# Mixture-of-experts stage: places in the token table by expert instead of by group, sorting and bringing back in sets of four experts

## The chip, the cores and the metric

The kernel runs on one core of one Trainium2 chip. Its time is the device time of one execution in microseconds (us). The core has a matrix engine (TensorE, in the profile PE for the matmuls and PEld for loading their stationary operand), VectorE (DVE), ScalarE (ACT), GpSimd (POOL) and SyncE (SP). Here SP issues nearly all loads of weights from HBM.

## The reference: what is computed

Two layers on 512 tokens of width 1024. A layer is a mixer (retention, differential attention and gated linear attention side by side, then an output projection) and a mixture of experts, both gated and added to the residual X. The change is in the mixture of experts alone:

```
def route(h, router_w, router_b):
    scores = sigmoid(h @ router_w);  biased = scores + router_b          # 32 experts in 8 groups of 4
    g_sel = argmax over groups of the sum of the group's 2 best biased scores
    idx = the 2 best experts inside that group;  gates = their scores, normalised
def moe(h, idx, gates, w_gate, w_up, w_down):                            # 1024x512, 1024x512, 512x1024 per expert
    u = silu(x_e @ w_gate[e]) * (x_e @ w_up[e])
    y_e = (u @ w_down[e]) * gates
    out[token] += y_e
```

All of it is fp32. An expert has 6 MiB of weights, so a layer reads 192 MiB for its 32 experts. With the inputs of the reference the eight groups of the first layer hold 115, 96, 85, 71, 54, 46, 31 and 14 tokens, those of the second 108, 105, 94, 64, 50, 41, 30 and 20. Ranked by their tokens, the experts of ranks 1, 6, 7, 16, 17 and 32 hold 82, 54, 49, 32, 29 and 1 in the first layer, and 93, 55, 47, 28, 27 and 3 in the second.

## The kernel before

**Routing.** `route(i)` finds the group of each token of tile i (four tiles of 128 tokens), `weigh(i)` the two experts and their gates. Matmuls with a triangle and with ones count the tokens of each group ahead of each token (`pc`), and a chain on VectorE ranks the eight groups by count. The four largest get 128 places each, the others 64: 768 places.

**Sorting the rows.** `Pt` is a 0/1 matrix of tokens by places. The normalised tokens, split in a rounded part `xh` and the rest `xl`, are multiplied by it: for each of two halves of the places (384 columns) and each of eight k, eight matmuls with 128x128 of `xh` or `xl` as the stationary operand, whose columns are read with a step of four elements (line 1358). The result `hs` stands for all places before the first expert starts.

**Experts.** A list `WHERE` sets their order: an expert of a large group (wide) and one of a small group (narrow) by turns. A wide expert's weights are split in two fp32r parts (a cast on ScalarE, a subtraction on VectorE: `split`), and each product is three fp32r matmuls (`three`), 72 of 512 columns per expert. A narrow expert takes fp32 weights as they are, and two 64-wide matmuls stand side by side in the array (`halved`); an fp32 matmul has two records in the trace. In the loop over experts, `gate_part(e+1)`, `down_part(e)` and `up_part(e+1)` follow each other, and after each quarter of one of these `step()` runs one step of what waits in the queue `apart`.

**Bringing back.** The four experts of a group add into one PSUM sum `ya`. After the fourth, `combine` scales it, splits it in two fp32r parts, and multiplies it by the transposed 0/1 matrix (built on VectorE from `srow`), eight small steps of two matmuls or four of four, which `step()` puts between the expert matmuls.

**Weights.** SP issues 1 MiB per DMA (line 1435), in the order in which the experts use them, into eight slots (two `ring`, four `wm`, two that are first `pre` and later `late`), each when its last reader is done with it. Instructions of the expert loop are recorded by a helper, line 122, so that line 122 stands for all of them.

**Rest.** If a group has more tokens than places, a loop after the experts takes the others in blocks of 128; with these inputs there are none.

Of the kernel before, what the change touches and what calls it, by code (L numbers as in the profile page):

```python
# [29 lines left out]
NWIDE = 4  # L30
CAPS = (128,) * NWIDE + (64,) * (NG - NWIDE)
OFFS = tuple(sum(CAPS[:r]) for r in range(NG))
PLACES = sum(CAPS)

WHERE = [(r, j) for w in range(NWIDE) for j in range(4) for r in (w, w + NWIDE)]
WHERE[-4:] = [(NWIDE - 1, 2), (NWIDE - 1, 3), (NG - 1, 2), (NG - 1, 3)]


def _constants():
    c, a = {}, {}  # L40
# [8 lines left out]
    c["ranks"] = np.broadcast_to(np.arange(8.0), (128, 8))  # L49
    c["scol"] = np.stack([OFFS[r] + p % CAPS[r] for r in range(8)], 1)  # L50
    c["caps"] = np.broadcast_to(np.array(CAPS, np.float64), (128, 8))
# [26 lines left out]
    a["places"] = np.broadcast_to(np.arange(float(PLACES // 2)), (128, PLACES // 2))  # L78
# [61 lines left out]
def hybrid_trunk(ctx: ExitStack, tc: tile.TileContext, x, c, positions, w_mod, b_mod, norm1_g, norm2_g, w_in,  # L140
# [89 lines left out]
    xmid = dr.tile([S, D])  # L230
# [138 lines left out]
    for l in range(depth):  # L369
        first = l == 0  # L370
        with ExitStack() as ps:
# [712 lines left out]
            places = rx.tile([128, PLACES // 2])  # L1084
            SP.dma_start(places, catt[:, AOFF["places"][0]:sum(AOFF["places"])])
# [26 lines left out]
            gate, grp = rt.tile([128, NT, NE]), p3.tile([128, NT, NG])  # L1112
# [14 lines left out]
            def route(i):  # L1127
# [14 lines left out]
                else:  # L1142

                    for n in range(2):
# [31 lines left out]
                V.tensor_scalar(grp[:, i], cst("gidx"), r1, None, op0=OP.is_equal)  # L1176

                T.matmul(pc[:, (i + 1) * NG:(1 + NT) * NG], cst("ones"),
                         grp[:, i, None, :].to_broadcast([128, NT - i, NG]), start=(i == 0), stop=False)
# [3 lines left out]
            def weigh(i):  # L1183
# [12 lines left out]
                V.scalar_tensor_tensor(two, two, IMM, sc, op0=OP.is_equal, op1=OP.mult)  # L1196
# [34 lines left out]
            for i in range(NT):  # L1231
                acc[i] = out_bank(i)
                second(i, 0)
                if i:
                    turn_x(i - 1, 1)
                    logits(i - 1, 0)
                turn_x(i, 0)
                second(i, 1)
                if i:
                    logits(i - 1, 1)  # L1240
                residual(acc[i], i, 1)
                SP.dma_start(xmid[i * 128:(i + 1) * 128], X[:, i])
# [10 lines left out]
            drain(ahead_, route(NT - 1))  # L1253


            gf = grp.rearrange("p i g -> p (i g)")
            T.matmul(pc[:, 0:NG], cst("ustrict"), gf[:, 0:NG], start=False, stop=False)
            T.matmul(pc[:, NG:NT * NG], cst("ustrict"), gf[:, NG:], start=False, stop=True)
# [4 lines left out]
            def over_groups(a, axis=1):  # L1263
                return a[:, None, :].to_broadcast([128, NG, NG]) if axis else a[:, :, None].to_broadcast([128, NG, NG])

            key, cmp_, rank = pt_([128, NG]), pt_([128, NG, NG]), pt_([128, NG])
            V.scalar_tensor_tensor(key, pc[:, NT * NG:(1 + NT) * NG], float(NG), cst("gidx"), op0=OP.mult, op1=OP.add)
            V.tensor_tensor(cmp_, over_groups(key), over_groups(key, 0), op=OP.is_gt)
            V.tensor_reduce(rank, cmp_, axis=AX.X, op=OP.add)

            at_rank, og, perm = pt_([128, NG, NG]), pt_([128, NG, NG]), pt_([128, NG])
            V.tensor_tensor(at_rank, over_groups(rank), over_groups(cst("ranks"), 0), op=OP.is_equal)
            V.tensor_tensor(og, at_rank, over_groups(cst("ranks")), op=OP.mult)
            V.tensor_reduce(perm, og, axis=AX.X, op=OP.add)
            permi = rt.tile([1, NG], I32)
            V.tensor_copy(permi, perm[0:1])

            tmp, tmp2 = pt_([128, NT, NG]), pt_([128, NT, NG])
            nth, rk, aw, cap, over, slot = [pt_([128, NT]) for _ in range(6)]
            V.tensor_mul(tmp.rearrange("p i g -> p (i g)"), pc[:, 0:NT * NG], gf)  # L1280
            V.tensor_tensor(tmp2, grp, rank[:, None, :].to_broadcast([128, NT, NG]), op=OP.mult)
            V.tensor_reduce(nth, tmp, axis=AX.X, op=OP.add)
            V.tensor_reduce(rk, tmp2, axis=AX.X, op=OP.add)
            V.tensor_scalar(cap, rk, NWIDE - 0.5, CAPS[-1] - CAPS[0], op0=OP.is_gt, op1=OP.mult)
            V.tensor_scalar(aw, rk, float(NWIDE), 0.0, op0=OP.subtract, op1=OP.max)
            V.tensor_scalar(cap, cap, float(CAPS[0]), None, op0=OP.add)
            V.scalar_tensor_tensor(aw, aw, CAPS[-1] / CAPS[0] - 1.0, rk, op0=OP.mult, op1=OP.add)
            V.tensor_tensor(over, nth, cap, op=OP.is_ge)
            V.scalar_tensor_tensor(slot, aw, float(CAPS[0]), nth, op0=OP.mult, op1=OP.add)
            slots = rt.tile([128, NT])  # L1290
            V.scalar_tensor_tensor(slots, over, 4.0 * S, slot, op0=OP.mult, op1=OP.add)
            Pt = rx.tile([128, NT, PLACES], F32R)
            HP = PLACES // 2
            slot2 = pt_([128, NT])
            V.tensor_scalar(slot2, slots, -float(HP), None, op0=OP.add)
            for c, of in enumerate((slots, slot2)):
                for i in range(NT):
                    V.tensor_scalar(Pt[:, i, c * HP:(c + 1) * HP], places, of[:, i:i + 1], None, op0=OP.is_equal)
            drain(weigh(NT - 2), weigh(NT - 1))

            gate4 = rt.tile([128, NT, 4])
            V.tensor_reduce(gate4, gate.rearrange("p i (g e) -> p i e g", e=4), axis=AX.X, op=OP.add)

            behind = rt.tile([128, NT])
            V.tensor_sub(nth, nth, cap)
            V.scalar_tensor_tensor(nth, rk, float(S), nth, op0=OP.mult, op1=OP.add)
            V.scalar_tensor_tensor(nth, nth, 1.0, over, op0=OP.add, op1=OP.mult)
            V.tensor_scalar(behind, nth, -1.0, None, op0=OP.add)
            nbi = rt.tile([1, NG + 1], I32)
            cnt, nbf, nbt = [pt_([128, NG]) for _ in range(3)]  # L1310
            V.tensor_tensor(og, at_rank, over_groups(pc[:, NT * NG:(1 + NT) * NG]), op=OP.mult)
            V.tensor_reduce(cnt, og, axis=AX.X, op=OP.add)
            V.tensor_sub(cnt, cnt, cst("caps"))
# [4 lines left out]
            V.tensor_copy(nbi[:, 0:NG], nbf[0:1])  # L1318
            V.tensor_reduce(nbt[:, 0:1], nbf, axis=AX.X, op=OP.max)
            V.tensor_copy(nbi[:, NG:NG + 1], nbt[0:1, 0:1])  # L1320
# [13 lines left out]
            npre = 2  # L1334
            after = {}

            def pre_done():

                spre.close()
                pre.clear()  # L1340
                wn = after["pool"] = pool(spre, f"wn{l}", "right")
                after["gt2b"] = wn.tile([128, D])
                A.dma_start(after["gt2b"], bcast(mods[l, 5 * D:6 * D], D))
                after["gt2h"] = wn.tile([128, 512])
                for n in range(2):
                    A.dma_start(after["gt2h"][64 * n:64 * n + 64], bcast(mods[l, 5 * D + 512 * n:5 * D + 512 * n + 512], 512, 64))
# [3 lines left out]


            hs = wm.tile([128, KD, PLACES])
            for c in range(2):
                for k in range(KD):
                    b = pbank("x", 3)[:, 0:HP]
                    for i in range(NT):
                        for n, xx in enumerate((xh, xl)):
                            T.matmul(b, xx[:, i].rearrange("p (q t k) -> p q k t", q=2, k=4)[:, k // 4, k % 4],
                                     Pt[:, i, c * HP:(c + 1) * HP], start=(i == 0 and n == 0), stop=(i == NT - 1 and n == 1))
                    dst = hs[:, k, c * HP:(c + 1) * HP]  # L1360
                    if k % 2:
                        V.tensor_scalar(dst, b, hcol[:, 0, k:k + 1], hcol[:, 1, k:k + 1], op0=OP.mult, op1=OP.add)
                    else:
                        A.activation(dst, b, AF.Identity, scale=hcol[:, 0, k:k + 1], bias=hcol[:, 1, k:k + 1])

            def window(r):

                nwin[0] += 1
                xT = wm.tile([128, 2, KD, 128], F32R, tag="exT")
                w = slice(OFFS[r], OFFS[r] + 128)  # L1370
                for h in ((0, 4), (4, 8)) if nwin[0] == 1 else ((0, 8),):
                    ks = slice(*h)
                    A.copy(xT[:, 0, ks], hs[:, ks, w])
                    V.tensor_sub(xT[:, 1, ks], hs[:, ks, w], xT[:, 0, ks])
                return xT

# [403 lines left out]
```

## Time and profile before

| | |
|---|---|
| time, median of 3 runs | 1844.78 us (1844.6 to 1845.76) |
| profiled execution: its time, its span | 1843.05 us, 1841.2 us |
| mean granted TensorE clock | 0.981 |
| PE busy | 1765.0 us (96%) |
| DVE, ACT busy | 1095.8 us (60%), 784.2 us (43%) |
| read from HBM | 501.73 MB |

The span is from the first to the last instruction; the execution's own time is 1.85 us longer. Busy time of PE has modelled ends, so that a busy PE is not PE at its peak. The mixture of experts takes about 550 us of each layer: from 419 to 971 us in the first, and from 1287 us to the end in the second.

### The profile page before, as it was taken

Reading aid. Unit: us, or ns where it says so; the run is one execution under the profiler, and the core shown is the slowest. Engines: PE = TensorE matmul, PEld = TensorE weight load, DVE = VectorE, ACT = ScalarE, POOL = GpSimd, SP = SyncE. Lnnn points to the kernel's source line nnn. Section 1 sums busy time; section 2 is a strip of 40 time slices with the busy share of each in tenths; the row PEclk is TensorE's granted clock in tenths of the full one; section 3 lists DMA queues with packets and bytes.
Section 4 is the critical chain, followed back from the end, with each engine's and each line's share of the span. In section 5 each row is a group of like instructions: output and inputs, shape, how many; then the busy total and the mean of one; then the engine's idle time right before and its main releaser. Section 6 shows DMA issues by size and latency. Waiting matters only on the chain. (4 is left out here: it accounts for less than half of the span.)

```text
span 1841.2 us, 28185 instructions
## 1 busy us (share of the span) xinstructions
PE 1765.0 (96%) x10891; PEld 1270.0 (69%) x10892; DVE 1095.8 (60%) x1968; ACT 784.2 (43%) x1207; POOL 89.4 (5%) x136
## 2 busy tenths in 40 slices
PE   5999999989999999999998999997999999999997
PEld 3866767768665666665748887986966666666673
DVE  3646664464547557566655778656455846756664
ACT  3344442343534443444523555443344444444350
POOL 1010000020000000000000110112000000000000
PEclk9999999998999999999998999998999999999998
DMA  9565547416999999999964211131789999999994
GB/s 333 166 213 191 171 160 226 164 73 253 359 423 378 392 423 367 415 422 353 423 247 141 70 46 47 54 124 51 308 358 422 369 403 422 367 415 419 362 420 179
DMA packets 115617, 512.12 MB, mean 278 GB/s; under 512 B 14978, under 2 KB 42896, under 8 KB 66320
## 3 DMA queue, kind: packets, MB, share of 16 engines
q1 hardware_dynamic: 111952, 504.93, 70.6%
q0 software_dynamic: 1072, 3.32, 0.5%
q10 hardware_dynamic: 2448, 1.94, 0.4%
q8 instruction: 90, 1.47, 0.3%
q14 instruction: 55, 0.45, 0.1%
HBM read 501.73 MB, written 8.42 MB: 277 GB/s over the span
## 5 line engine op out<-in xcount | busy, mean ns | idle before, releaser
L122 DVE TENSOR_TENSOR H<-R,H 128x1024 fp32r<-128x1024 f32 x368 | 431.4, 1221 | 108.9 <-ACT H L122 108.4
L122 ACT CAST H<-R 128x1024 fp32r<-128x1024 f32 x368 | 363.8, 1048 | 47.5 <-DMA R<-in_w_down_dram 28.7
L579 PEld LDWEIGHTS a<-H,u 128*128 128x128 f32 x1728 | 216.5, 190 | 45.0 <-issue 42.2
L579 PE MATMUL a<-H,u 128*128 128x256 f32 x1728 | 245.7, 290 | 0.0
L122 PE MATMUL y<-H,euT 128*128 128x512 f32 x768 | 188.4, 399 | 1.0 <-DVE euT L122 1.0
L122 PE MATMUL g<-H,exT 128*128 128x512 f32 x720 | 183.9, 402 | 0.0
L122 PE MATMUL u<-H,exT 128*128 128x512 f32 x720 | 177.1, 400 | 0.0
L122 PEld LDWEIGHTS y<-H,euT 128*128 128x128 f32 x768 | 141.6, 188 | 46.1 <-ACT H L122 9.2
L122 PEld LDWEIGHTS u<-H,exT 128*128 128x128 f32 x720 | 132.6, 188 | 54.3 <-issue 22.5
L122 PEld LDWEIGHTS g<-H,exT 128*128 128x128 f32 x720 | 131.4, 188 | 36.1 <-issue 8.5
L122 DVE SCALAR_TENSOR_TENSOR eu<-u,u,es 128x256 f32<-128x256 f32 (+1 forms) x62 | 37.9, 612 | 190.3 <-PE u L122 190.3
L122 PE MATMUL g<-R,u 128*64 128x256 f32 x1024 | 126.8, 386 | 0.0
L122 PE MATMUL y<-R,euT 128*64 128x512 f32 x512 | 121.2, 602 | 1.1 <-ACT euT L122 1.1
L122 PE MATMUL u<-R,u 128*64 128x256 f32 x1024 | 118.9, 383 | 0.0
L122 DVE TENSOR_TENSOR u<-u,x 128x512 f32<-128x512 f32 x128 | 84.4, 684 | 45.7 <-PE x L122 45.4
L122 PEld LDWEIGHTS u<-R,u 128*64 128x64 f32 x1024 | 70.1, 137 | 45.3 <-issue 13.9
L122 ACT COPY euT<-x 128x256 f32<-128x256 f32 x32 | 11.9, 373 | 209.9 <-PE x L122 189.3
L122 PEld LDWEIGHTS g<-R,u 128*64 128x64 f32 x1024 | 66.9, 136 | 46.3 <-issue 15.4
L122 PE MATMUL x<-eyh,ePT 128*128 128x512 f32 (+1 forms) x256 | 75.1, 460 | 9.2 <-DVE u L122 5.8
L122 ACT CAST euT<-x 128x512 fp32r<-128x512 f32 x32 | 18.7, 584 | 150.6 <-PE x L122 150.5
L122 PEld LDWEIGHTS y<-R,euT 128*64 128x64 f32 x512 | 32.3, 136 | 63.6 <-issue 52.2
L122 PEld LDWEIGHTS x<-eyh,ePT 128*128 128x128 f32 (+1 forms) x256 | 33.7, 192 | 51.2 <-DVE u L122 31.0
(597 smaller groups left out, 2289.4 us busy)
## 6 DMA issues: line engine op xcount, KB each, us to landing
R<-in_w_gate_dram SPq DMA_DIRECT2D x128, 1024.0 KB
R<-in_w_up_dram SPq DMA_DIRECT2D x128, 1024.0 KB
R<-in_w_down_dram SPq DMA_DIRECT2D x128, 1024.0 KB
M<-in_w_mod_dram SPq DMA_DIRECT2D x80, 512.0 KB
R<-in_w_in_dram SPq DMA_DIRECT2D x20, 1024.0 KB
slab<-in_w_mod_dram SPq DMA_DIRECT2D x16, 512.0 KB
R<-in_w_in_dram SPq DMA_DIRECT2D x24, 256.0 KB
R<-in_w_out_dram SPq DMA_DIRECT2D x4, 1024.0 KB
```

Source lines behind the costliest of these rows:

```text
L122: return self.tc.keep_in_program_order(f(*args, **kw))
L579: T.matmul(acc[i // 2][:, i % 2], a[q][:, k, tk], hl[:, w, k], start=(i % 2 == 0 and q == 0 and k == 0 and n3 == 0), stop=(i % 2 == 1 and ...
```

## The change

Places are given to experts, not to groups. The 32 experts are ranked by their tokens; the six largest get 128 places each, the next ten 64 and the last sixteen 32. They stand in eight sets of four, `(128, 32, 64, 32)` six times and `(64, 32, 64, 32)` twice, and are computed in that order. The table of places before was one matrix of 768 columns for all; now it is one of 256 (or 192) columns for each set, made by `select(s)` while the first expert of the set ahead of it is at work. An expert with 32 places uses four 32-wide matmuls side by side. The sums of a 128- or 64-place expert are scaled and split right after it (`finish`), those of four 32-place experts are put together in four blocks; `combine(s)` then adds all the blocks of a set in one PSUM sum for each tile of tokens. The weights have six slots (`ring` and `wm`) after three first ones (`pre`) are given up.

```
-NWIDE = 4
-CAPS = (128,) * NWIDE + (64,) * (NG - NWIDE)
+SETS = ((128, 32, 64, 32),) * 6 + ((64, 32, 64, 32),) * 2
...
-            drain(ahead_, route(NT - 1))
+            drain(chained(ahead_, weigh(NT - 2)), chained(route(NT - 1), weigh(NT - 1)))
...
+            V.tensor_scalar(cmp_, krow, kcol, None, op0=OP.is_gt)
+            V.tensor_reduce(rank, cmp_, axis=AX.X, op=OP.add)
+            V.tensor_scalar(at_rank, cst("ranks")[0:NE], rank, None, op0=OP.is_equal)
+            b = bt()
+            T.matmul(b[0:1, 0:NE], cst("pidx")[0:NE], at_rank, start=True, stop=True)
...
+                T.transpose(b[0:NE, i * 128:(i + 1) * 128], place[:, i], ident)
+            A.copy(placeT, b[0:NE])
...
+                T.matmul(b[:, i * NE:(i + 1) * NE], placeT[:, i * 128:(i + 1) * 128], at_rank, start=True, stop=True)
+            V.tensor_scalar(placeR.rearrange("p i e -> p (i e)"), b[:, 0:NT * NE], BIG, None, op0=OP.add)
...
-            npre = 2
+            npre = 3
...
-            hs = wm.tile([128, KD, PLACES])
-            for c in range(2):
-                for k in range(KD):
...
+            def select(s):
...
+                for _, cap, o, r in mine:
+                    V.tensor_tensor(Pt[:, :, o:o + cap], cst("iota")[:, None, 0:cap].to_broadcast([128, NT, cap]),
+                                    placeR[:, :, r:r + 1].to_broadcast([128, NT, cap]), op=OP.is_equal)
+                yield
...
+                for k in range(KD):
+                    b = pbank("x", 3)[:, 0:w]
+                    for i in range(NT):
+                        for n, xx in enumerate((xh, xl)):
+                            T.matmul(b, xx[:, i].rearrange("p (q t k) -> p q k t", q=2, k=4)[:, k // 4, k % 4], Pt[:, i, 0:w],
+                                     start=(i == 0 and n == 0), stop=(i == NT - 1 and n == 1))
...
+                    yield
...
+                        for h in range(128 // cap):
+                            T.matmul(b[cap * h:cap * (h + 1), j:j + 1], Pt[:, i, o:o + cap].bitcast(F32), gateR[:, i, r:r + 1],
...
-                place = oldest("R8", [("ring", nr), ("wm", mr_)] + [("pre", npre)] * len(pre) + [("late", lr)] * len(late))
+                place = oldest("R8", [("pre", npre)] * len(pre) + [("ring", nr), ("wm", mr_)])
...
+            def apart_(out, a, cap, columns, start, stop, turned_=0):
+                n = 128 // cap
+                for h in range(n):
+                    w = columns((h - turned_) % n)
+                    T.matmul(out[cap * h:cap * (h + 1), 0:w.shape[-1]], a, w, start=start, stop=stop)
...
+            def step():
+                for todo in (later, ahead_of):
+                    if todo and next(todo[0], todo) is todo:
+                        todo.popleft()
...
+            def places_of(cap, which, n):
+                b = pbank("x", 3)
+                T.matmul(b, which, prow, start=True, stop=True)
+                PT = after["pool"].tile([128, NT, 128], F32R, tag=f"PT{n}")
...
+                V.tensor_scalar(PT.rearrange("p i t -> p (i t)"), b, cst("scol")[:, j:j + 1], None, op0=OP.is_equal)
...
+            def combine(s):
+                yield from of_quarters(s)
+                for i in range(NT):
+                    add(done[s], i)
+                    yield
...
-            src = _Ahead(pieces(items), lambda: 4)
+            src = _Ahead(pieces(items), lambda: 1)
...
+                if e % 4 == 0 and s + 1 < len(SETS):
+                    ahead_of.append(select(s + 1))
...
+                if e % 4 == 3 and e + 1 < ne:
+                    later.append(combine(s))
```

The first place is on PE, inside the down product of the first 128-place expert (`y`, weights `H`). Before, four runs of six matmuls follow each other there, and the narrow expert's up product (`u`, 64 wide) comes next:

```order
L122 MATMUL y_4699<-H_866_4704,euT_4723 128x512 x6
L122 MATMUL y_4699<-H_867_4711,euT_4723 128x512 x6
L122 MATMUL y_4699<-H_871_4728,euT_4723 128x512 x6
L122 MATMUL y_4699<-H_872_4735,euT_4723 128x512 x6
L122 MATMUL u_4781<-R_875_4751,u_817_4385 64x256 x8
```

Now, in the same product, a burst of `select` for the set after (`x` from `Pt`, with `xh` and `xl` as the two stationary operands by turns) stands between two runs of six, and so on through the product and through the 32-place expert's gate and up ahead of it and behind it:

```order
L128 MATMUL y_4769<-H_873_4744,euT_4717 128x512 x6
L128 MATMUL x_4779<-Pt_4681,u_685_3812 128x256
L128 MATMUL x_4779<-Pt_4681,u_686_3813 128x256
L128 MATMUL x_4779<-Pt_4681,u_685_3812 128x256
L128 MATMUL x_4779<-Pt_4681,u_686_3813 128x256
L128 MATMUL x_4779<-Pt_4681,u_685_3812 128x256
L128 MATMUL x_4779<-Pt_4681,u_686_3813 128x256
L128 MATMUL x_4779<-Pt_4681,u_685_3812 128x256
L128 MATMUL x_4779<-Pt_4681,u_686_3813 128x256
L128 MATMUL y_4769<-H_877_4770,euT_4717 128x512 x6
```

The sorting moved from ahead of all experts into the first expert of each set, eight matmuls at a time.

The second place is on PE too, where the sums of a set come back: what is new is a burst for one tile of tokens (`yh` the scaled sums of a 128-place and of a 64-place expert, `PT` their transposed 0/1 matrices) inside the next set's first 32-place gate (`g`, 32 wide):

```order
L128 MATMUL g_5326<-R_962_5301,hs_4696 32x128 x8
L128 MATMUL x_5335<-yh_893_4876,PT_902_4965 128x512
L128 MATMUL x_5336<-yh_898_4905,PT_902_4965 128x512
L128 MATMUL x_5335<-yh_893_4876,PT_902_4965 128x512
L128 MATMUL x_5336<-yh_898_4905,PT_902_4965 128x512
L128 MATMUL x_5335<-yh_934_5138,PT_937_5153 128x512
L128 MATMUL x_5336<-yh_934_5138,PT_937_5153 128x512
L128 MATMUL x_5335<-yh_934_5138,PT_937_5153 128x512
L128 MATMUL x_5336<-yh_934_5138,PT_937_5153 128x512
L128 MATMUL g_5326<-R_962_5301,hs_4696 32x128 x8
```

Before, such a burst came once per group, not per set, and had two matmuls (wide) or four (narrow); now it has eight, and 16 in every second set, with the 32-place blocks.

## Rows read from the trace of the kernel before

**Rows 1.** The page: span.
```profile
span 1841.2 us, 28185 instructions
```

**Rows 2.** Windows, first layer: routing, sorting, experts, end; length, then busy us by engine, clock, DMA share, GB/s.
```profile
399.60:418.90 19.30, 7.19 (x44) 6.28 (x42) 13.93 (x76) 5.45 (x12) 5.41 (x5) 0.69 0.07 28
418.90:454.00 35.10, 35.01 (x150) 33.26 (x150) 15.20 (x40) 10.49 (x16) 3.04 (x4) 0.93 0.66 263
454.00:958.40 504.40, 500.97 (x2662) 325.82 (x2661) 304.40 (x327) 222.91 (x271) 0.00 (x0) 1.00 0.96 386
958.40:971.00 12.60, 4.94 (x17) 2.23 (x16) 9.98 (x19) 8.29 (x21) 0.00 (x0) 0.69 0.29 80
```

**Rows 3.** Windows: one stretch amid the experts at full load.
```profile
500.00:520.00 20.00, 20.00 (x109) 12.86 (x105) 12.53 (x12) 10.40 (x13) 0.00 (x0) 1.00 1.01 423
```

**Rows 4.** Groups by form, PE, 400 to 980 us: busy us, mean ns of one.
```profile
L122 PE MATMUL y<-H,euT 128*128 128x512 f32 x384 | 94.2, 399 | 0.5 <-DVE euT L122 0.5
L122 PE MATMUL g<-H,exT 128*128 128x512 f32 x360 | 91.9, 402 | 0.0
...
L122 PE MATMUL g<-R,u 128*64 128x256 f32 x512 | 63.4, 386 | 0.0
L122 PE MATMUL y<-R,euT 128*64 128x512 f32 x256 | 60.6, 602 | 0.5 <-ACT euT L122 0.5
...
L1358 PE MATMUL x<-u,u 128*128 128x384 f32 x128 | 31.6, 411 | 3.2 <-DVE u L1298 3.2
L122 PE MATMUL x<-eyh,ePT 128*128 128x512 f32 x64 | 22.2, 428 | 0.0
L122 PE MATMUL x<-u,eu 128*128 128x128 f32 x96 | 18.5, 302 | 0.5 <-DVE eu L122 0.2
L122 PE MATMUL x<-eyh,ePT 64*128 64x512 f32 x64 | 15.2, 486 | 4.9 <-DVE u L122 3.1 <-ACT eyh L122 1.4 <-DVE eyh L122 0.3
...
L1609 PE MATMUL x<-u,u 4*64 4x4 f32 x16 | 0.6, 197 | 0.0
```

**Rows 5.** Timeline on PE: two runs of 32-wide matmuls; start us, us.
```profile
118.23 0.62 PE L695 MATMUL l<-QF,KF 128*32 128x128 f32 x16
118.67 0.61 PE L322 MATMUL m<-M,u 128*32 128x256 f32 x8
```

**Rows 6.** Timeline on ACT and DVE: two results of the sorting one after the other.
```profile
441.27 0.67 ACT L1364 ACTIVATE u<-x,u 128x384 f32<-128x384 f32 x1 [3.06 <-PE x L1358]
443.14 0.68 DVE L1362 TENSOR_SCALAR u<-x,u 128x384 f32<-128x384 f32 x1 [3.06 <-PE x L1358]
```

**Rows 7.** Groups by form, PEld, 400 to 980 us.
```profile
L122 PEld LDWEIGHTS y<-H,euT 128*128 128x128 f32 x384 | 70.8, 188 | 23.0 <-ACT H L122 4.6 <-DVE euT L122 1.8 <-issue 1.2
L1358 PEld LDWEIGHTS x<-u,u 128*128 128x128 f32 x128 | 31.3, 330 | 3.4 <-issue 3.3
L122 PEld LDWEIGHTS x<-u,eu 128*128 128x128 f32 x96 | 15.0, 205 | 9.3 <-issue 4.6 <-DVE eu L122 1.8 <-DVE u L122 1.1
```

**Rows 8.** The page's groups: fp32r matmuls of 256 columns in the mixer.
```profile
L579 PE MATMUL a<-H,u 128*128 128x256 f32 x1728 | 245.7, 290 | 0.0
```

**Rows 9.** Timeline on PE: a burst of bringing back between 64-wide matmuls.
```profile
936.49 0.73 PE L122 MATMUL x<-eyh,ePT 128*128 128x512 f32 x2
937.16 1.08 PE L122 MATMUL g<-R,u 128*64 128x256 f32 x8
938.17 0.73 PE L122 MATMUL x<-eyh,ePT 128*128 128x512 f32 x2
```

**Rows 10.** Timeline, the last tile's group on DVE, and the first sorting matmul.
```profile
414.04 0.23 DVE L1176 TENSOR_SCALAR u<-u,r 128x8 f32<-128x8 f32 x1
...
418.99 0.68 PE L1358 MATMUL x<-u,u 128*128 128x384 f32 x1 [3.19 <-DVE u L1298]
```

**Rows 11.** Timeline, from the last expert's sum to the next layer's first matmul.
```profile
958.46 0.69 DVE L122 TENSOR_TENSOR es<-y,u 128x512 f32<-128x512 f32 x1 [7.25 <-PE y L122]
...
971.69 0.58 PE L450 MATMUL t<-at,u 128*128 128x128 f32 x1 [5.43 <-DVE at L429]
```

More of the change, by code (lines that the diff above doesn't have):

```diff
@@ L28, with _order @@
 START = GV, DQ, DK
[L30 to L36 removed]
+SETS = ((128, 32, 64, 32),) * 6 + ((64, 32, 64, 32),) * 2
+KINDS = (128, 64, 32)
+BIG = 1024.0
+def _order():
+    ex = [(s, n, c) for s, cs in enumerate(SETS) for n, c in enumerate(cs)]
+    rank = {e[:2]: r for r, e in enumerate(sorted(ex, key=lambda e: (-e[2], e[:2])))}
+    return [(s, c, sum(SETS[s][:n]), rank[s, n]) for s, n, c in ex]
+ORDER = _order()
+CAPS = [c for s, c, o, r in sorted(ORDER, key=lambda e: e[3])]
 def _constants():
@@ L1273, in hybrid_trunk @@
[L1273 to L1281, printed above, removed]
@@ L1289, in hybrid_trunk @@
[L1289 to L1298, printed above, removed]
@@ L1299, in hybrid_trunk @@
[L1299 to L1313, printed above, removed]
+            ccol, kcol, krow, rank, cmp_, at_rank = [pt_([NE, n]) for n in (1, 1, NE, 1, NE, NE)]
+            V.tensor_copy(ccol, b[0:NE, 0:1])
+            V.scalar_tensor_tensor(kcol, ccol, float(NE), cst("pidx")[0:NE], op0=OP.mult, op1=OP.subtract)
@@ new lines, in hybrid_trunk @@
+            b = bt()
+            for i in range(NT):
+                T.matmul(b[:, i * NE:(i + 1) * NE], gateT[:, i * 128:(i + 1) * 128], at_rank, start=True, stop=True)
+            V.tensor_copy(gateR.rearrange("p i e -> p (i e)"), b[:, 0:NT * NE])
+            prow, oner = rt.tile([NE, S], F32R), rt.tile([NE, NE], F32R)
+            b = bt()
+            T.matmul(b[0:NE], at_rank, placeT, start=True, stop=True)
+            A.copy(prow, b[0:NE])
+            G.tensor_copy(oner, ident[0:NE, 0:NE])
@@ L1341, in pre_done @@
                 wn = after["pool"] = pool(spre, f"wn{l}", "right")
[L1342 to L1346, printed above, removed]
+                for c_ in KINDS:
+                    w, m = D * c_ // 128, 128 // c_
+                    for a_ in range(m if c_ == 32 else 1):
+                        g_ = after[c_, a_] = wn.tile([128, w])
+                        for n in range(m):
+                            o = 5 * D + w * ((n - a_) % m)
+                            A.dma_start(g_[c_ * n:c_ * (n + 1)], bcast(mods[l, o:o + w], w, c_))
@@ new lines, in select @@
+                    yield
+                b = pbank("x", 3)[:, 0:4]
+                for j, (_, cap, o, r) in enumerate(mine):
+                    for i in range(NT):
+                        for h in range(128 // cap):
+                            T.matmul(b[cap * h:cap * (h + 1), j:j + 1], Pt[:, i, o:o + cap].bitcast(F32), gateR[:, i, r:r + 1],
+                                     start=(i == 0 and j == 0), stop=(i == NT - 1 and j == len(mine) - 1))
+                gc = gcols[s] = wm.tile([128, 4], tag="gc", bufs=2)
@@ L1556, in combine_last @@
+            def combine(s):
+                yield from of_quarters(s)
+                for i in range(NT):
+                    add(done[s], i)
+                    yield
+                del done[s]
+            def combine_last(s):
                 if l + 1 < depth:
                     preload("natural_log_exp_and_others")
-                PT = back(r)
-                yfs = [gain_y(ya, n, wm.tile([128, 512], tag=("es", "eu")[n]), wide_) for n in range(2 if wide_ else 1)]
-                yhs = [parts(yf) for yf in yfs]
+                for _ in of_quarters(s):
+                    pass
@@ new lines, in hybrid_trunk @@
+                            for i in range(NT):
+                                G.tensor_scalar(diag[:, i], ident, ob[:, i:i + 1], None, op0=OP.mult)
+                            b = pbank("x", 3)
+                            T.matmul(b, cst("ones"), diag.rearrange("p i t -> p (i t)"), start=True, stop=True)
+                            PTb = after["pool"].tile([128, NT, 128], F32R, tag="PT0")
+                            V.tensor_scalar(PTb.rearrange("p i t -> p (i t)"), b, cst("pidx"), None, op0=OP.is_equal)
@@ new lines, in hybrid_trunk @@
+                            for q in range(4):
+                                T.transpose(b[:, q], u_.rearrange("p (q t k) -> p q k t", q=2, k=2)[:, q // 2, q % 2], ident)
+                            ub = wm.tile([128, 2, KD, 128], tag="exT")[:, 0, 0:4]
+                            A.copy(ub, b)
+                            ya = pbank("y", 1, [128, 2, 512])
+                            for q, raw in enumerate(raws(w_down)):
+                                for k in range(2):
+                                    for n in range(2):
+                                        T.matmul(ya[:, n], ub[:, 2 * q + k], raw[:, k * D + n * 512:k * D + n * 512 + 512],
+                                                 start=(q == 0 and k == 0), stop=(q == 1 and k == 1))
@@ L1740, in hybrid_trunk @@
+                            yhs = []
+                            for n in range(2):
+                                yf = after["pool"].tile([128, 512], tag="eyf")
+                                V.tensor_mul(yf, ya[:, n], after[128, 0][:, n * 512:(n + 1) * 512])
+                                yhs.append(parts(yf, f"yh0{n}"))
+                            for i in range(NT):
+                                add([(128, PTb, yhs)], i)
                 if l + 1 < depth:
```

419 lines of the change are left out of this document (200 added, 219 removed).

## Prediction

> **What bounds the kernel now.** I began with the windows by stage [rows 2]. The reader is to see that a layer's experts take 504.4 us, and that PE is busy for 501.0 of them at full clock while the DMA engines are at 0.96. Nothing idles there that could be given back; DVE (304) and ACT (223) have room. The second thing to see is how close the loads are: at full load 423 GB/s [rows 3], so 1 MiB in 2.48 us, and the 192 pieces of a layer in 476 us. The sorting ahead of the experts is 35.1 us of PE, during which the slots fill and the loads then stop (263 GB/s). So the change has to be read as a bill on PE, with the loads as a floor some 60 us under the present sum of sorting and experts (539.5 us). All sums are made against the profiled execution, 1843.05 us with a span of 1841.2 [rows 1], 0.1% under the median of the runs shown.
>
> **The bill on PE, per layer.** Groups by form give each price [rows 4]; a group's busy time holds the modelled ends of its runs, so differences under some 10 us are not to be trusted.
>
> - *Experts.* A 128-place expert has three parts of 24 matmuls: 94.2/16 = 5.9 us for down, 91.9/15 = 6.1 for gate (up stands between them), 18.0 in all. A 64-place one has 4.0 (63.4/16) and 3.8 (60.6/16), 11.6 in all. For 32 places the nearest row is the mixer's 32-wide run [rows 5]: 16 records, which are two groups of four fp32 matmuls of 128 columns, in 118.67 - 118.23 = 0.44 us, so 0.22 per k. Gate and up have eight k, down has four of twice the columns: 3 x 1.76 = 5.3, with run ends 5.6. Ten 128-place experts go (-180), six 64-place ones go (-70), sixteen of the new kind come (+90): **-160**. Bounds of the new kind: 5.3, and 8.8 if their weight columns, which gate and up read with a step of two, come at half the rate: -165 to -109. I stay near the low end, because transposes read their stationary operand with that step and pay little for it (load 205 ns against 188 [rows 7]).
> - *Sorting.* 128 matmuls become 8 sets x 64 = 512. Columns fall from 384 to 256 each, but I don't think that helps. Two results of eight matmuls come 1.87 us apart [rows 6], 0.234 us per matmul, though a 512-column matmul of the experts costs 94.2/384 = 0.245. What stands behind it is the load of the stationary operand with its step of four: 330 ns mean against 188, and busy 31.3 of the 31.6 us [rows 4, 7]. So each of the 512 costs 0.247 still (31.6/128): 126 us, **+95**. The lower bound is the fp32r matmul of 256 columns with a contiguous operand, 245.7/1728 = 0.142 [rows 8]: 73 us, +41.
> - *Bringing back.* Per layer 96 matmuls of 128 rows at 0.245 (23), 160 of 64 rows at 15.2/64 = 0.24 at most and half of that where two run side by side (30), 128 of 256 columns at 0.142 (18): 72, less the present 22.2 + 15.2: **+34** (+20 to +45).
> - *Placement and gates.* 32 new matmuls of 512 columns spread each expert's places over the rows: **+8**. The gates of the places come from 352 matmuls of one column, 704 records at 0.6/16 = 0.037 as the 64-wide ones there: 26, less about 4 now: **+22** (+10 to +30). Transposes fall from 96 to 60 at 0.19: **-7**.
> - *Visits.* Each burst between matmuls of another tile width costs something beside its matmuls: from 937.16 to 938.83 (938.17 and the two matmuls' 0.66) pass 1.67 us for eight records of 0.124 and two of 0.245, which leaves 0.19 [rows 9]. Visits go from 48 to about 120 (56 of sorting, 28 of bringing back, 32 of placement, 7 of gates): **+14**, and a first strided load that nothing hides in each burst of sorting makes it **+18** (+10 to +30).
>
> The sum is **+10 us per layer on PE** (-70 to +85, were all bounds to go one way). The saving in experts is eaten by sorting.
>
> One rule speaks on the largest term. The Trainium skill (TensorE: Matmul & The Clock Gate, LDWEIGHTS) gives the load of a stationary operand as columns over 1.2 GHz, an estimate of 107 ns for 128 columns whatever their step; by it the sorting would be no dearer than the contiguous row and the sum -44. The same skill (Advanced Engine Details and Errata, SBUF Cachelines) says that accesses need two hits on a 16-byte line for full speed, which a step of four fp32 misses and a step of two keeps; the 330, 205 and 188 ns of the trace agree with this one.
>
> **The slots.** DVE, ACT and SP lose work or have room: 120 splits fewer a layer. What does not even out is the order. All sorting, and nearly all of bringing back, falls to the first expert of a set. Call A the stretch of gate(32), down(128), up(32) in a set: 9.5 us of experts, 8 x 1.87 of sorting, visits 2.4, gates 3, transposes and placement 2, and bringing back 4 x 2 us, in every second set 6 more: about 41 us. Its loads are 15 us, and then six slots are full. The next three iterations take 3.9 + 1.8 + 3.9, 1.8 + 3.8 + 1.8 and 6.1 + 1.8 + 5.9 = 31 us on PE; of their 18 pieces six lie ready and twelve have to come, 12 x 2.48 = 30 us, after the first slot is freed and with the way from issue to use, about 33. PE then waits 2 us at least; since the loads lag most on the short 32-place parts and are ahead again only in A, I take 4 us for each of eight sets: **+32 per layer** (0, if the slots cover it, to +64). Before, a wide and a narrow expert by turns took 18.0 + 11.6 = 29.6 us for 29.8 us of loads, with eight slots: nothing to even out.
>
> **Both ends.** The routing now waits for `weigh` and then goes six times between PE, DVE and ACT (counts, rank, transposes, regrouping, 0/1 matrix) where it went twice: 414.04 to 418.99 now [rows 10]; I take **+5** (+2 to +9). After the last expert, four placements, eight small casts and four bursts of 16 matmuls follow, against four bursts of four: 958.46 to 971.69 now [rows 11], **+7** (+3 to +12). ACT issues 19 gain loads where it issued three, in the first expert: **+1**.
>
> Per layer 10 + 32 + 5 + 7 + 1 = +55, for two layers +110: 1843 + 110 = 1953, on the scale of the runs **1955 us**.
>
> **Rivals.**
> *The loads, not PE, set the stage, and it is faster.* The mechanism is the sorting's matmul: at the contiguous 0.142 us each set's A falls by 6 us and the set comes nearer to its loads. That gives 55 - 54 = +1 per layer, and with even sets no waits for slots, -31: 1843 - 62, about 1780. It decides at 0.14 us per sorting matmul if the waits stay, at 0.20 if they go. For it: the columns do fall by a third. Against it: busy 31.3 of 31.6 us of loads, which 256 columns don't shorten. Chance 0.09. The LDWEIGHTS rule of the Trainium skill (TensorE: Matmul & The Clock Gate), weighed above, would have it so.
> *PE alone counts.* The six slots cover A's unevenness: 55 - 32 = +23 per layer, 1890. For it: the loads had 0.04 to spare on average. Against it: eight slots become six while the sets become uneven. Chance 0.25.
> *The forecast*, 1955, own range 1915 to 2000: chance 0.50.
> *Worse.* Waits at their upper bound and 32-place weights at half rate: +32 + 50 more per layer, about 2100; either alone 2020 to 2055. Chance 0.12.
> *It does not do what it says.* Were an expert to have more tokens than places, the block loop would run with 6 MiB loaded beside nothing, 15 us of loads plus its matmuls, 30 us or more for each; the counts of the inputs leave three places at the tightest rank (29 of 32), so it stays empty. What is left, 0.04, is a change of no size.
>
> **How the numbers follow.** The likeliest case gives 1955. The range 1870 to 2015 takes in the case of PE alone and the forecast, and part of the worse one; 0.1 stays out below and 0.1 above. A measurement of this kernel tells about 0.2% from no change. Faster 0.10, within 0.2% 0.03, slower 0.87.
>
> **What would show it.** Sorting: 512 matmuls a layer at 0.23 to 0.25 us, their loads busy nearly all of it; at 0.14 my largest term is wrong. The 32-place parts: 1.8 us each without interruption. The windows: PE near 100% and DMA well under 0.9 in each A, then DMA at 1.0 and PE with gaps that weights end in the three iterations behind it; a stage with PE full throughout is the second rival. The experts with their sorting should take 580 us where sorting and experts take 539.5 now. Wrong altogether would be a stage near 500 us with DMA at 1.0.

## The result and the profile after

The changed kernel takes **2160.61 us** (median of 4 runs, 2154.89 to 2162.45) where the kernel before takes 1844.69 us (1842.37 to 1845.76): ratio 1.171, 95% interval 1.169 to 1.173. It is slower, as forecast, but by 316 us where I said 110, and far outside the range. The profiled execution takes 2154.89 us, its span is 2153.0 us. The page, with the line on the core's clock, shows PE busy for longer, at a smaller share of the span, and at a lower granted clock (before: 1765.0 us, 96%, 0.981):

```profile
span 2153.0 us, 39387 instructions
PE 1907.8 (89%) x16315; PEld 1396.0 (65%) x16316; DVE 1030.2 (48%) x2278; ACT 645.0 (30%) x1215; POOL 95.4 (4%) x186
...
core 0: 2153.0 us, clock 0.925
```

The windows of the first layer, in the columns of [rows 2]: routing, from the first sorting matmul to the last down product, and the end. Then the first set in three pieces: its stretch A (32-place gate, 128-place down and 32-place up, with sorting between, and the first 3 us of the 64-place gate that follows), the rest of the three iterations behind it, and the end of the last 128-place up with most of the sums brought back:

```profile
399.60:423.70 24.10, 14.65 (x71) 10.57 (x70) 15.99 (x80) 6.02 (x13) 4.99 (x4) 0.56 0.12 44
423.70:1107.40 683.70, 595.04 (x5429) 412.98 (x5432) 280.72 (x509) 160.41 (x284) 5.60 (x28) 0.90 0.75 297
1107.40:1130.40 23.00, 15.15 (x77) 10.00 (x69) 14.28 (x29) 11.97 (x28) 0.40 (x1) 0.83 0.29 90
...
470.80:502.00 31.20, 31.14 (x293) 26.44 (x293) 16.59 (x36) 9.40 (x16) 0.00 (x0) 0.95 0.52 188
502.00:542.80 40.80, 31.74 (x305) 19.32 (x304) 16.59 (x23) 13.77 (x23) 0.00 (x0) 0.95 1.00 410
542.80:554.20 11.40, 11.12 (x71) 6.29 (x69) 5.87 (x12) 0.00 (x0) 0.00 (x0) 0.87 0.66 243
```

The same stretch of the kernel before, sorting and experts in one window:

```profile
418.90:957.80 538.90, 535.38 (x2808) 359.08 (x2810) 319.60 (x367) 233.41 (x286) 3.04 (x4) 1.00 0.94 379
```

The stage is 144.8 us longer per layer (683.7 against 538.9), and the DMA engines, busy to 0.94 before, are at 0.75 (0.52 in A). Of the 144.8 us, 85 are PE's idle time (683.7 - 595.0 = 88.7 against 538.9 - 535.4 = 3.5) and 60 are busy time. Much of that busy time is not work: a mean clock of 0.90, where the engine has only its full level (2.4 GHz) and half of it (1.2 GHz), means 2 x 0.10 x 683.7 = 137 us at half level, in which up to 68 us are lost. An estimate from the trace sums the intervals from one PE start to the next, each at the mean that its form of matmul has at full level: 542 us of work with the ends of runs (534 before), 53 lost at half level (1 before) and 89 of waits (3 before). So work +8, clock +52, waits +85.

The set shows where. A and the bringing back run at PE's pace, 31.2 + 11.4 us, and the DMA engines move 188 and 243 GB/s in them. Between them 40.8 us go at the pace of the loads (share 1.00, 410 GB/s), and PE lacks 9.1 us. The timeline on PE in that piece, where the columns are as in [rows 5] and the brackets hold the idle time ahead and what ended it:

```profile
513.35 1.94 PE L128 MATMUL yn<-R,euTn 128*64 128x512 f32 x8 [1.08 <-DMA R<-in_w_down_dram]
515.75 1.94 PE L128 MATMUL yn<-R,euTn 128*64 128x512 f32 x8 [0.46 <-DMA R<-in_w_down_dram]
518.33 1.12 PE L128 MATMUL u<-R,hs 128*32 128x128 f32 x32 [0.65 <-DMA R<-in_w_up_dram]
519.38 0.49 PE L128 MATMUL x<-u,u 32*128 32x512 f32 x1
520.74 1.14 PE L128 MATMUL u<-R,hs 128*32 128x128 f32 x32 [0.87 <-DMA R<-in_w_up_dram]
524.29 0.49 PE L128 MATMUL g<-H,exT 128*128 128x512 f32 x1 [2.42 <-ACT H L128]
525.55 4.30 PE L128 MATMUL g<-H,exT 128*128 128x512 f32 x11 [0.77 <-DVE H L128]
...
532.58 1.44 PE L128 MATMUL g<-H,exT 128*128 128x512 f32 x5 [0.76 <-DVE H L128]
533.95 1.93 PE L128 MATMUL yn<-R,euTn 128*32 128x256 f32 x32
...
540.18 0.51 PE L128 MATMUL u<-H,exT 128*128 128x512 f32 x1 [1.30 <-ACT H L128]
541.44 1.65 PE L128 MATMUL u<-H,exT 128*128 128x512 f32 x5 [0.76 <-DVE H L128]
```

The short parts wait for loads. Then the gate of the next 128-place expert begins, and its first piece is split (cast on ACT, subtraction on DVE) only when PE already wants it: 2.42 us, then 0.77. ACT shows why, and the window of this gate shows the clock:

```profile
523.20 1.99 ACT L128 CAST H<-R 128x1024 fp32r<-128x1024 f32 x2 [4.12 <-DMA R<-in_w_gate_dram]
...
524.00:534.00 10.00, 8.18 (x29) 5.58 (x33) 5.07 (x5) 4.07 (x6) 0.00 (x0) 0.83 1.01 420
```

The cast itself had waited 4.12 us for its load, so the 2.42 us are a late load with a cast behind it. From 524.29 to 533.95 a gate of 6 us takes 9.7, with two more waits for splits and a clock of 0.83. Over the stage, the waits of PE by what ended them (us in total, times, longest):

```profile
PE yn L128 <- DMA R<-in_w_down_dram: 18.1, 17, 2.8
PE u L128 <- DMA R<-in_w_up_dram: 16.1, 19, 1.5
PE u L1423 <- ACT H L1417: 13.2, 2, 12.3
PE g L128 <- ACT H L128: 11.5, 5, 2.4
PE g L128 <- DVE H L128: 6.7, 10, 0.8
PE g L128 <- DMA R<-in_w_gate_dram: 6.2, 8, 1.5
PE u L128 <- ACT H L128: 6.0, 5, 1.5
```

Loads end 40 us and splits some 28 (with a small group that is not shown: `u`, ended by DVE, 3.8). Of these 28, by the rows on ACT, 14 stand behind a cast that had waited for its load, as above, and 14 behind casts that followed other work on ACT without a break. So late loads are behind some 55 us. One wait of 12.3 us stands alone: the first expert's up, whose split sits in ACT's queue behind the loads of the gains. The timeline on ACT and its queue:

```profile
447.96 1.28 ACT L1500 ACT_TABLE_LOAD   x1
...
449.88 11.83 ACTq L1350 DMA_DIRECT2D u<-u  x16
462.06 1.99 ACT L1417 CAST H<-R 128x1024 fp32r<-128x1024 f32 x2 [12.20 <-DMA u<-u]
```

What the forecast put on PE's bill is there at its price. Groups by form on PE and PEld, first layer, the sorting and the three kinds of bringing back:

```profile
L128 PE MATMUL x<-Pt,u 128*128 128x256 f32 x320 | 81.1, 398 | 3.8 <-DVE Pt L128 3.8
L128 PE MATMUL x<-Pt,u 128*128 128x192 f32 x128 | 32.5, 400 | 1.0 <-DVE Pt L128 1.0
L128 PE MATMUL x<-yh,PT 64*128 64x512 f32 x160 | 30.9, 466 | 0.3 <-DVE PTq L128 0.3
L128 PE MATMUL x<-yh,PT 128*128 128x512 f32 x96 | 29.3, 428 | 0.0
L128 PE MATMUL x<-yq,PTq 128*128 128x256 f32 x128 | 20.6, 307 | 0.0
L1375 PE MATMUL x<-Pt,u 128*128 128x256 f32 x64 | 15.3, 415 | 0.0
...
L128 PEld LDWEIGHTS x<-Pt,u 128*128 128x128 f32 x448 | 109.1, 328 | 13.3 <-DVE Pt L128 6.0 <-issue 3.3 <-DVE hs L128 2.6
```

512 sorting matmuls take 81.1 + 32.5 + 15.3 = 129 us, 0.25 each, and those of 192 columns cost as much as those of 256. The load (328 ns) sets the price and not the columns, as e2 shows.

### The profile page after: what moved, and what is told of

It is laid out like the page before. It is cut to its first block, busy times and chain, and to the rows that moved or that the text cites. A ratio compares the mean times of both kernels' runs of the same rounds, so it can differ in the third digit from the quotient of the medians.

```text
span 2153.0 us, 39387 instructions
## 1 busy us (share of the span) xinstructions
PE 1907.8 (89%) x16315; PEld 1396.0 (65%) x16316; DVE 1030.2 (48%) x2278; ACT 645.0 (30%) x1215; POOL 95.4 (4%) x186
## 5 line engine op out<-in xcount | busy, mean ns | idle before, releaser
L128 PE MATMUL x<-Pt,u 128*128 128x256 f32 (+1 forms) x896 | 227.2, 398 | 10.7 <-DVE Pt L128 10.6
L128 PEld LDWEIGHTS x<-Pt,u 128*128 128x128 f32 x896 | 218.2, 328 | 27.4 <-DVE Pt L128 12.9
L128 DVE TENSOR_TENSOR H<-R,H 128x1024 fp32r<-128x1024 f32 x128 | 155.2, 1224 | 98.2 <-ACT H L128 96.3
L128 PE MATMUL yn<-R,euTn 128*32 128x256 f32 (+1 forms) x1344 | 156.2, 462 | 36.0 <-DMA R<-in_w_down_dram 34.6
L128 PE MATMUL g<-R,hs 128*32 128x128 f32 (+1 forms) x2560 | 156.1, 321 | 12.0 <-DMA R<-in_w_gate_dram 12.0
L128 PE MATMUL u<-R,hs 128*32 128x128 f32 (+1 forms) x2560 | 142.6, 315 | 25.1 <-DMA R<-in_w_up_dram 25.1
L128 ACT CAST H<-R 128x1024 fp32r<-128x1024 f32 x128 | 131.6, 1042 | 60.9 <-DMA R<-in_w_gate_dram 43.4
L128 PE MATMUL g<-H,exT 128*128 128x512 f32 x240 | 86.8, 513 | 36.2 <-ACT H L128 22.5
L128 PE MATMUL x<-yh,PT 64*128 64x512 f32 (+1 forms) x512 | 116.2, 449 | 0.3 <-DVE PTq L128 0.3
L128 PE MATMUL u<-H,exT 128*128 128x512 f32 x240 | 68.5, 421 | 19.4 <-ACT H L128 11.8
```

Source lines behind the costliest of these rows:

```text
L128: return self.tc.keep_in_program_order(f(*args, **kw))
```

## The experiments

All times are medians, of four runs each, of two for e9 and e10; the ratio is to the kernel before on the same chip. "Idle" and "clock" are those of PE from the first sorting matmul to the last down product of the first layer.

| kernel | us | ratio (95%) | stage | idle | clock |
|---|---|---|---|---|---|
| changed kernel | 2160.6 | 1.171 (1.169-1.173) | 683.7 | 88.7 | 0.90 |
| e1 sorting spread | 2074.1 | 1.123 (1.121-1.125) | 638.9 | 54.7 | 0.94 |
| e2 contiguous operands | 2058.3 | 1.115 (1.113-1.117) | 632.6 | 96.6 | 0.91 |
| e3 gains by GpSimd | 2138.4 | 1.159 (1.157-1.161) | 667.2 | 82.0 | 0.93 |
| e4 no gate columns | 2124.7 | 1.151 (1.148-1.153) | 664.4 | 106.8 | 0.94 |
| e5 two pieces ahead | 2140.2 | 1.159 (1.155-1.164) | 675.9 | 78.5 | 0.89 |
| e6 = e1 + e2 + e3 | 1957.8 | 1.062 (1.060-1.064) | 578.1 | 57.0 | 0.96 |
| e7 = e6 + e5 | 1910.0 | 1.035 (1.032-1.038) | 558.8 | 42.3 | 0.95 |
| e8 before, contiguous | 1833.3 | 0.994 (0.992-0.996) | 532.5 | 3.9 | 1.00 |
| e9 four slots | 2246.1 | 1.217 (1.205-1.229) | 737.5 | 119.9 | 0.88 |
| e10 an eighth of the sorting | 2028.8 | 1.099 (1.094-1.105) | 617.6 | 105.0 | 0.90 |

**e1: the sorting spread over three experts.**

```
                         V.tensor_sub(xT[:, 1, k], xf, xT[:, 0, k])
-                    yield
+                    for _ in range(4):
+                        yield
```

> The eight bursts of sorting for the next set lie four steps apart, over the first three experts of a set, instead of one step apart in the first; nothing else changes. Theory (uneven sets: the loads stop while the sorting fills the first stretch, PE then waits for weights and loses its clock): waits per layer fall from about 80 to some 30 us and the loss at half clock from about 50 to 20, so 2160 - 2 x 80 = 2000 us, 1960 to 2040; DMA share near 0.9 throughout a set. Rival (six slots are too few for the short 32-place parts wherever the sorting lies): the waits stay, 2120 us or more.

2074 us: half of what the theory said, twice what its rival allowed. The same instructions, in another order, save 86 us, so unevenness has a price; but 54.7 us of idle time stay. The waits on PE of this run show of what kind:

```profile
PE u L1424 <- ACT H L1418: 12.7, 2, 11.8
PE y L128 <- DVE H L128: 7.6, 10, 0.8
PE u L128 <- DMA R<-in_w_up_dram: 7.1, 7, 1.5
...
PE u L128 <- ACT H L128: 5.6, 5, 1.2
```

Waits that end with a load fall from 40 to 12 us (with 5.2 in two groups that are not shown); those that end with a split hardly change in sum, 28 to 24, but they are others. None stands behind a late load any more (14 before). Those behind other work on ACT go from 14 to 24, 10 of them in the 128-place down (`y`), which had none while sorting stood between its runs. So the spread mends the late loads, and splits that the sorting had covered come to light.

**e2: contiguous operands for the sorting.** The rounded rows `xh`, and their rests `xl` in the same way, are written in the order in which the sorting reads their columns:

```
-                A.activation(xh[:, i], X[:, i], AF.Copy, scale=r2)
+                for n in range(2):
+                    cs_ = slice(n * 512, (n + 1) * 512)
+                    A.activation(by_k(xh[:, i, cs_]), of_k(X[:, i, cs_]), AF.Copy, scale=r2)
...
-                            T.matmul(b, xx[:, i].rearrange("p (q t k) -> p q k t", q=2, k=4)[:, k // 4, k % 4], Pt[:, i, 0:w],
+                            T.matmul(b, xx[:, i].rearrange("p (q k t) -> p q k t", q=2, k=4)[:, k // 4, k % 4], Pt[:, i, 0:w],
```

> The rounded rows and their rests are stored so that the 128 columns of a stationary operand of the sorting lie side by side instead of 16 bytes apart; as many matmuls. Theory (the step of four is what a sorting matmul costs): 0.237 us per matmul becomes 0.12 to 0.145, 512 x 0.1 = 50 us less PE work per layer, all of it in the first stretch of each set, 2160 - 100 = 2060 us (2030 to 2080), load mean 190 ns. Rival (the load does not depend on the step, each matmul has that price for another reason): 2150 to 2165 us, load mean 330 ns.

2058 us, as the theory has it. Groups by form on PE and PEld, first layer:

```profile
L128 PE MATMUL x<-Pt,u 128*128 128x256 f32 x320 | 46.4, 289 | 3.8 <-DVE Pt L128 3.8
L128 PE MATMUL x<-Pt,u 128*128 128x192 f32 x128 | 17.1, 277 | 1.0 <-DVE Pt L128 1.0
L1385 PE MATMUL x<-Pt,u 128*128 128x256 f32 x64 | 9.4, 316 | 0.0
...
L128 PEld LDWEIGHTS x<-Pt,u 128*128 128x128 f32 x448 | 58.0, 191 | 13.4 <-DVE Pt L128 6.0 <-issue 3.3 <-DVE hs L128 1.8
```

The load falls from 328 to 191 ns and the sorting from 129 to 73 us. The time falls by 51 us per layer, about that and no more: idle time goes from 88.7 to 96.6. Shorter sorting does not bring fewer waits.

**e3: the gain loads issued by GpSimd.**

```
-                        A.dma_start(g_[c_ * n:c_ * (n + 1)], bcast(mods[l, o:o + w], w, c_))
+                        G.dma_start(g_[c_ * n:c_ * (n + 1)], bcast(mods[l, o:o + w], w, c_))
```

> The 19 loads of gains per layer are issued by GpSimd instead of ScalarE. Theory (ScalarE's queue is held for 11.8 us by 16 issues while the first expert's split waits behind them): 12 us less per layer, 2160 - 24 = 2136 us. Rival (the split would have waited for its weights anyway): 2155 us or more.

2138 us, 11 us per layer, the theory's. The wait of 12.3 us is gone from PE's waits.

**e4: without the gate columns.** The loop of one-column matmuls is left out and the gates are set to a constant.

> The 352 matmuls of one column per layer are left out; the gates of all places are the constant 0.5. Theory (they cost their own time and also the clock, which falls to half behind them): 16 x 2.3 = 37 us of their own and 20 to 35 us of half clock, 2090 to 2105 us, and no stretch at half clock right behind the place where they stood. Rival (the clock falls for another reason): 2115 to 2130 us.

2125 us: in time their own 2.3 us in each set and nothing more, as the rival has it. Its reason is not borne out. In the changed kernel the clock falls to half level right behind these columns in six of the eight sets, with PE busy without a break ahead; without them every fall in the stage has idle time of PE just ahead of it or in it. The changed kernel (two rows of PE and a window), then the same 16 records of the 64-place gate in e4:

```profile
494.76 2.34 PE L128 MATMUL x<-u,Pt 128*128 128x1 f32 x88
498.91 3.21 PE L128 MATMUL g<-R,hs 128*64 128x256 f32 x16
498.10:501.50 3.40, 3.40 (x28) 1.90 (x25) 1.07 (x2) 0.00 (x0) 0.00 (x0) 0.50 0.69 251
...
493.09 1.95 PE L128 MATMUL g<-R,hs 128*64 128x256 f32 x16
```

The time at half level goes from 137 to 80 us (2 x 0.06 x 664.4). PE is busy for 37 us less, 18 of them the columns' own. The other 19 are lost again in waits: PE's idle time rises by 18 us, and the waits that end with a load go from 40 to 55.

**e5: two pieces ahead.**

```
-            src = _Ahead(pieces(items), lambda: 1)
+            src = _Ahead(pieces(items), lambda: 2)
```

> Of the changed kernel, only the depth to which pieces of weights are fetched and split ahead of their matmuls goes from one to two. Theory (a split made one piece ahead comes too late behind the short 32-place pieces: some 28 us per layer of PE's waits end with a split): 15 to 25 us less per layer with the clock that follows, 2110 to 2130 us, and few waits that end with a split. Rival (these waits are late weights in another dress): 2150 us or more, the waits then end with a load.

2140 us, between the two: 10 us less idle time and no better clock. While the loads are late, a split made earlier waits for its load: split-ended waits behind other work on ACT fall from 14 to 5 us, those behind a late load stay (14 and 16).

**e6 and e7: e1, e2 and e3 together, then two pieces ahead as well.**

> Spread sorting, contiguous stationary operands and the gain loads on GpSimd together. If the three are separate costs: 2160 - 86 - 102 - 22 = 1950 us (1930 to 1975). If the spread and the contiguous operands mend the same waits: 1980 to 2020 us.

> The same three with splits two pieces ahead. Theory (splits one piece ahead are a wait of their own, now that the loads come in time): 35 to 60 us below the run before it, 1890 to 1930 us. Rival (PE's work and the loads set it by then): less than 15 us below it.

1958 us: the three costs add (86 + 102 + 22 = 210, measured 203). On top of them the second piece ahead is worth 48 us, not 20, since most loads come in time now (they end 17 us of waits in e6, 40 in the changed kernel). The stage then takes 558.8 us, 20 more than before, with 42.3 us idle:

```profile
426.10:984.90 558.80, 516.52 (x5430) 342.82 (x5432) 277.35 (x509) 158.67 (x284) 5.61 (x28) 0.95 0.90 361
```

**e8: the kernel before, with contiguous operands.** The edit of e2 on its 128 sorting matmuls.

> The kernel before with contiguous stationary operands of its sorting, 128 matmuls of 384 columns per layer. Theory (the step costs): 0.247 becomes about 0.19 us per matmul, 7 us less per layer, 1830 us (1826 to 1836). Rival (at 384 columns the matmul itself takes as long): 1843 to 1848 us.

1833 us, faster than both kernels: 0.61% under the kernel before, interval 0.44 to 0.78, which is 5 us per layer where the theory has 7. Group by form on PEld:

```profile
L1368 PEld LDWEIGHTS x<-u,u 128*128 128x128 f32 x128 | 24.0, 203 | 4.4 <-issue 3.4 <-ACT u L1374 0.9
```

**e9: four slots**, with `mr_=2` for `mr_=4`.

> The changed kernel with four slots of 1 MiB for weights instead of six. Theory (the slots are the stock that PE lives on behind the first stretch of a set): two slots less are 5 us less stock for each of eight sets, 40 us per layer, 2210 to 2270 us, DMA share in the sorting stretch lower still. Rival (not the slots but the order of splits holds the loads): 2160 to 2185 us.

2246 us: 43 us per layer for two slots, where eight sets by two loads of 2.5 us are 40. The slots are the stock on which PE lives behind A: waits that end with a load rise from 40 to 70 us. That the sum is so close is partly chance, as the stage of the profiled run is 54 us longer, of which 31 are idle time and most of the rest is clock (0.88).

**e10: an eighth of the sorting.** In all sets but the first, `range(NT)` becomes `range(1)` and `xl` is left out.

> The changed kernel with one of eight matmuls of the sorting in all sets but the first (the experts then get one tile's rounded rows only, so seven eighths of that sum are left out): 392 matmuls less per layer, 392 x 0.237 = 93 us of PE work. If its work alone is its price, as with the contiguous operands: 2160 - 186 = 1975 us (1950 to 1995). If the unevenness that it makes has a price beside the work: 1850 to 1930 us. If the loads then bind, the DMA share in the sets is over 0.95.

2029 us, which neither line foresaw: 66 us per layer come back for 93 us of work taken away. PE's idle time grows to 105 us, and the DMA share in the stage is 0.83, so the loads do not bind as a whole either:

```profile
426.90:1044.50 617.60, 512.56 (x5041) 323.96 (x5040) 276.82 (x509) 159.52 (x284) 5.02 (x28) 0.90 0.83 329
```

That corrects my theory of e1: it is not the length of A that makes the waits. From the first matmul of the 64-place gate to the end of the next 128-place up, the first set takes the same time in both kernels (the changed kernel, then e10), though what lies ahead of it, from the end of the up before, falls from 30.3 to 20.8 us:

```profile
498.90:547.50 48.60, 39.54 (x338) 23.80 (x335) 18.23 (x26) 13.77 (x23) 0.00 (x0) 0.90 0.98 399
497.00:545.60 48.60, 39.02 (x339) 23.71 (x336) 19.13 (x29) 13.88 (x23) 0.00 (x0) 0.91 0.98 395
...
PE y L128 <- DVE H L128: 9.2, 18, 1.1
```

In the five sets that another 128-place expert follows, these iterations take 46.5 to 48.8 us in the changed kernel and 48.0 to 48.7 in e10: they go at the pace of their loads and splits whatever A is. Waits that end with a load stay (40 and 44 us). Most of the 16 us of new idle time is in A, in the 128-place down, which without sorting between its runs waits 11 us for its own splits (the last row, and 1.8 ended by ACT). Work moved out of A into the iterations (e1) fills their idle time: they grow by 3.5 us on average, and what lies ahead of them falls by 9. Work taken out of A (e2, e10) gives its own time or less.

## Why the prediction was wrong, step by step

**The direction and its mechanism were right.** The change costs time because sorting now takes 512 matmuls at the price of 128, and sets are uneven for the loads.

**The bill on PE held, in part by luck.** I said +10 us per layer (-70 to +85, though the bounds of the terms add up to -83 and +92); the sum of intervals at full clock gives +8. Single terms missed by 8 or 9 us in both directions. Its terms: sorting +97 (129 - 31.6) for +95. The price is the step of the stationary operand: 328 ns against 191 with nothing changed but the order of columns (e2). The Trainium skill (TensorE: Matmul & The Clock Gate, LDWEIGHTS) gives the load by its columns alone, which would have both at one price; the measurement decides against it here, and with the section SBUF Cachelines of Advanced Engine Details and Errata, where a different 16-byte line at each access costs time. Bringing back is +43 in groups' busy time (30.9 + 29.3 + 20.6 - 37.4), with run ends and some half clock in it, for +34. The gate columns took 8 x 2.3 = 18 us per layer where I counted 26 before taking off 4. A 32-place gate or up without interruption takes two runs of 1.05 us, 2.1 where I took 1.76 from the mixer's row: 6.1 us an expert for 5.6, 8 us per layer; half rate is ruled out.

**Both ends held.** The routing is 4.8 us longer (24.1 against 19.3) for +5, and from the last down product to the next layer's first matmul (1130.35) it is 23.0 us where it was 13.9: +9 for +7.

**"ACT issues 19 gain loads ... +1" failed.** I took the price of the issues and not of what stands behind them: the split of the first expert's up is next in ACT's queue and waits 12.2 us, and e3 gives 11 us per layer back with nothing but another engine as issuer.

**"The slots ... +32 per layer" is the step that failed most.** The picture was right, its size not. Of the first set's 83.4 us, A and the bringing back, put at 41 us, take some 40. The three iterations behind, put at 35 us (31 of PE and 4 of waits), take some 44 (48.6 less 4.8 of bringing back between), with 9 us of waits and up to 5 of half clock. I took the loads' lag for little more than half of what it is: loads end 40 us of waits per layer, and 14 more end with a split whose cast had waited for its load, 55 in all against 32. That the slots and the order make these waits is shown by e9, where two slots less make the 40 into 70, and by e1, where the order alone makes the 55 into 12. I left the splits out: the queue ahead of PE has one piece of depth where it had four (the diff shows it), so that a 128-place part that follows a short one starts with a split that comes too late, 14 us per layer. With the 13 of the gains and some 7 that end with work on DVE and ACT beside the splits, idle time is 89 us, up by 85. e5 shows that depth by itself is worth only 10 us per layer while the loads are late, and e7 that it is worth 24 once they are not. The two waits cover for one another, so neither can be priced alone.

**"All at full clock" was never said and is the other half of the miss.** The experts' prices in my bill came from a stage whose clock was 1.00, that of sorting from one at 0.93 [rows 2]. In the changed kernel 137 us of a layer's stage ran at half level, worth about 52 us by the sum of intervals, and the sum of my forecast has no term for it. In the first set the clock fell behind the gate columns (0.50 in 498.1 to 501.5), amid the waits (0.83 in 524 to 534) and behind them (0.87 in 542.8 to 554.2). Over the stage it is higher in the denser e6 and e7 (0.96, 0.95). But e10 (idle 105, clock 0.90) and e4 (106.8, 0.94) show that idle time alone does not fix it, and e4 that the loss cannot simply be added to the waits: 57 us less at half level came with 18 us more of waiting. What one wait costs in clock is read from the rows and not isolated by a run.

Together: 144.8 + 4.8 + 9.1 = 159 us in the first layer, 155.9 per layer in the span, against 55.

**The rivals.** "The loads set the stage, and it is faster" rested on a sorting matmul of 0.142 us; e2 makes it just that (73/512 = 0.143), and the kernel is still 1.115 times as long, because the waits do not go with A (idle 96.6 us). "PE alone counts" is refuted by 88.7 us of idle time. "Worse" had its mechanism half right, waits past their upper bound of +64, without half rate of the weights; clock and gains took it further.

**What stays open.** In e7 sorting and experts take 20 us more than before with some 42 us less work (492 against 534 by the sum of intervals); 42 us are idle there and some 25 are clock. Waits that end with a split lead again (19 us, loads 14), with three buffers for split pieces. No run has more buffers or more than six slots, so what they would give is not known. Nor is it known what exactly lets the clock fall in a given set.

## What to carry to other kernels

A price per instruction holds at the clock and the density it was read at. Before adding up terms from a dense stage, ask whether the stage will still be dense: here the stretches at half clock came amid short waits and behind bursts of one-column matmuls. Where the time of the work and that of the loads are close, look at each stretch between two refills of the buffers by itself: moving work from the stretch that PE sets into the one that loads set gave 43 us per layer with no instruction removed. And a DMA issue on a compute engine costs what stands behind it in that engine's queue.

## What the runs showed of the hardware

- The order of columns alone changes the load of a 128x128 stationary operand from 328 to 191 ns (e2), and the matmul behind it from 0.25 to 0.143 us; at 384 columns from 330 to 203 ns (e8).
- 16 DMA issues on ACT held its queue for 11.83 us, 0.74 us each; with the same issues on GpSimd the wait of 12.3 us behind them is gone (e3).
- The granted clock fell to half level (1.2 GHz) behind 88 records of one-column matmuls (2.3 us) in six of eight sets, with PE busy throughout, and at none of these places without them (e4). In one of them 16 records of a 64-place gate then took 3.21 us, against 1.95 in e4.
